# One encoder layer on one core: the mix as seven half-size products, and the first layer norm by token rows

## The chip, the cores and the metric

The kernel runs on one core of one Trainium2 chip. The metric is the device time of one execution, in microseconds (us); before the change the median of three runs is 2267.95 us (2264.13 to 2268.24). One execution was also taken by the hardware profiler, and all rows below come from it.

## The reference

One layer of a bidirectional encoder: 512 tokens, 2048 channels, everything in float32.

```python
proj = h @ w_in[i]                                   # 512x2048 @ 2048x4608
...                                                  # 8 windowed heads (oa), 8 dilated heads (ob)
ya = rms_norm(oa.reshape(b, s, A_Q), gn_a[i])
yb = rms_norm(ob.reshape(b, s, B_QKV), gn_b[i])
mix = jnp.concatenate([ya, yb], axis=-1) @ w_o[i]    # 512x2048 @ 2048x2048
h = layer_norm(ALPHA * h + mix, ln1_g[i], ln1_b[i])
ff = jnp.square(jax.nn.relu(h @ w1[i])) @ w2[i]      # 2048 -> 8192 -> 2048
ple = (p[i] @ w_ple[i]) * jax.nn.sigmoid(h @ w_ple_gate[i])
h = layer_norm(ALPHA * h + ff + ple, ln2_g[i], ln2_b[i])
```

## The kernel before

Each float32 operand is split into a rounded part (name ending in h, made by ScalarE with a Copy) and the rest (ending in l, made by VectorE with a subtract). A product is three matmuls: high by high, high by low, low by high.

**Phase 1** runs 36 projection units of 48 matmuls each; the attention heads are interleaved with them. Its weights come in pieces of 1024 columns that are split in halves of 512.

**The mix** follows: 16 output blocks on the windowed half `yA`, 16 on the dilated half `yB`, 24 matmuls a block, 768 in all, with channels on the partitions. The last head's work is strewn between the first blocks. `Norm` (`add`, `shift`, `take`, `stats`) gathers the first layer norm's sums during the second half: sums over channels are matmuls with a vector of ones (`col_sums`, L265), and a row of results is spread over the partitions by matmuls too (`spread`, L281). Then 96 matmuls of the PLE product run, `norm` scales the 16 blocks (L465, L466, L501), and SyncE stores them to `h_d` (L502).

**The gate, w1 and w2** use Strassen's scheme (`strassen`, L602): the product of tokens and weights is cut in halves of tokens (th), of contraction and of columns, and seven products of half size replace eight. One call handles half of the output columns: 28 steps of 12 matmuls of 512 columns, in the order of `STEPS`, an entry (product, contraction piece). VectorE makes the sums of weights that the products need (L616, L617, L625, L634) and the low halves (L599). The sums of activations, the factors, come from `h_factors` (L536), which reloads quarters of h from `h_d`, adds them and splits them (L545 to L574). A finished product is added into the output quarters it belongs to (`quarters`), and a full quarter goes to `gated`, which multiplies the sigmoid by the PLE quarter, turns h by matmuls with the identity (L694) and adds it (L695).

Gate is two such calls, w1 eight, w2 eight. The last w2 call feeds the second layer norm: `finish` (L761) runs once for each half of tokens, the half th=1 when product 4 ends, th=0 when product 2 ends, which is the last in `STEPS`.

Each engine works through its own list in order, and a dependent instruction holds up all behind it. Weights are loaded into rings of a few buffers: SyncE issues those of the rings "r" and "q", GpSimd those of "k".

## Time and profile before

| | before |
|---|---|
| median of 3 runs | 2267.95 us |
| the profiled execution, its own time | 2262.9 us |
| its span, first to last instruction | 2261.1 us |
| TensorE busy in the span | 2144.7 us (95%) |
| VectorE, ScalarE, GpSimd busy | 1612.5, 1061.6, 124.3 us |
| mean granted TensorE clock | 0.982 |

Names in the rows: PE is TensorE, PEld its weight load, DVE VectorE, ACT ScalarE, POOL GpSimd, SP SyncE. "a<-b" is output from inputs. Durations of neighbouring instructions overlap; the pitch, from one start to the next, is what an instruction costs in a row of equals.

### The profile page before, as it was taken

The page shows a single profiled execution, that of the slowest core. Times are in us where ns is not written, and L with a number is a line of the kernel's source. Part 1 is how long each engine was busy: PE and PEld are TensorE (multiplying, and loading weights), DVE is VectorE, ACT ScalarE, POOL GpSimd, SP SyncE. Part 2 cuts the span into 40 slices and gives each one's busy share as a digit, 9 for nine tenths or more (in the row PEclk, how much of TensorE's full clock was granted, in tenths as well). Part 3 has the DMA queues.
Part 4 walks back from the last instruction along what each step waited for, and adds up shares of the span by engine and source line. Part 5 has one row for each costly group of instructions (what it writes and reads, how often), then busy time and mean ns, then how long its engine had stood idle before and what let it go on. Part 6 is the DMA issues. An engine that isn't in the chain of part 4 may idle for free.

```text
span 2261.1 us, 26072 instructions
## 1 busy us (share of the span) xinstructions
PE 2144.7 (95%) x9672; PEld 1757.3 (78%) x9672; DVE 1612.5 (71%) x1969; ACT 1061.6 (47%) x1372; POOL 124.3 (5%) x192
## 2 busy tenths in 40 slices
PE   9999999999995799999999999998899999999994
PEld 7888888888884588888888888776777787787783
DVE  7666655566475988776876877777677776777787
ACT  5554444343234444454555455455445555455331
POOL 0000000000003000000000000000011011001000
PEclk9999999999998899999999999999999999999997
DMA  6212212224225775565565566567669679678552
GB/s 225 75 66 76 84 66 84 84 100 138 99 88 209 269 271 202 202 230 180 190 229 177 196 214 204 190 221 250 202 186 285 182 206 277 181 210 289 187 197 82
DMA packets 124544, 401.60 MB, mean 178 GB/s; under 512 B 13024, under 2 KB 24288, under 8 KB 124416
## 3 DMA queue, kind: packets, MB, share of 16 engines
q1 hardware_dynamic: 88544, 285.51, 36.7%
q0 software_dynamic: 23584, 85.06, 13.4%
q10 hardware_dynamic: 12288, 29.36, 3.5%
q8 instruction: 76, 1.25, 0.2%
q14 instruction: 52, 0.43, 0.1%
HBM read 329.63 MB, written 70.25 MB: 177 GB/s over the span
## 4 chain that ended last, share of the span: by engine, by line
PE 76%; DMA 9%; DVE 9%; issue 3%; ACT 2%; DVEq 0%; SPq 0%; ACTq 0%
PE u L72 9%; PE u L71 9%; PE a L656 9%; PE u L73 9%; PE a L653 9%; PE a L655 8%; DMA wr<-in_w 5%; PE b L656 4%; PE b L653 4%; PE b L655 4%; DVE wl L599 4%; PE c L656 2%; PE c L653 2%; PE c L655 2%; DMA qs<-s_d 2%
## 5 line engine op out<-in xcount | busy, mean ns | idle before, releaser
L598 ACT ACTIVATE wh<-wr 128x1024 fp32r<-128x1024 f32 x288 | 303.8, 1059 | 345.2 <-PE a L655 194.0
L599 DVE TENSOR_TENSOR wl<-wr,wh 128x1024 fp32r<-128x1024 f32 x288 | 350.2, 1221 | 96.5 <-ACT wh L598 93.3
L64 ACT ACTIVATE wh<-raw 128x512 fp32r<-128x512 f32 x216 | 135.7, 629 | 282.2 <-PE u L72 267.3
L65 DVE TENSOR_TENSOR wl<-raw,wh 128x512 fp32r<-128x512 f32 x216 | 150.8, 699 | 160.8 <-ACT wh L64 129.0
L598 ACT ACTIVATE wh<-wk 128x1024 fp32r<-128x1024 f32 x144 | 152.6, 1060 | 179.3 <-PE b L655 89.5
L71 PE MATMUL u<-xh,wh 128*128 128x512 f32 x576 | 227.8, 395 | 5.6 <-ACT xh L64 5.6
L73 PE MATMUL u<-xh,wl 128*128 128x512 f32 x576 | 225.7, 392 | 0.0
L72 PE MATMUL u<-xl,wh 128*128 128x512 f32 x576 | 225.6, 392 | 0.0
L599 DVE TENSOR_TENSOR wl<-wk,wh 128x1024 fp32r<-128x1024 f32 x144 | 175.6, 1222 | 66.2 <-ACT wh L598 66.1
L634 DVE TENSOR_TENSOR wk<-wr,wk 128x1024 f32<-128x1024 f32 x72 | 88.2, 1224 | 97.1 <-DMA wr<-in_w 91.2
L653 PE MATMUL a<-wh,s1h 128*128 128x512 f32 x288 | 114.8, 399 | 30.7 <-DMA qh<-h_d 29.3
L71 PEld LDWEIGHTS u<-xh,wh 128*128 128x128 f32 x576 | 108.9, 189 | 27.1 <-ACT xh L64 5.6
L653 PE MATMUL b<-wh,s5h 128*128 128x512 f32 x288 | 116.6, 405 | 12.1 <-ACT wh L598 12.1
L73 PEld LDWEIGHTS u<-xh,wl 128*128 128x128 f32 x576 | 108.7, 189 | 22.7
L656 PE MATMUL b<-wl,s5h 128*128 128x512 f32 x288 | 117.2, 407 | 9.3 <-DVE wl L599 9.3
L72 PEld LDWEIGHTS u<-xl,wh 128*128 128x128 f32 x576 | 108.9, 189 | 22.0 <-DVE xl L65 0.4
L656 PE MATMUL c<-wl,s2h 128*128 128x512 f32 x288 | 113.3, 393 | 6.0 <-DVE wl L599 5.7
L656 PE MATMUL b<-wl,s3h 128*128 128x512 f32 x288 | 113.5, 394 | 4.1 <-DVE wl L599 3.9
L656 PE MATMUL a<-wl,s1h 128*128 128x512 f32 x288 | 114.8, 399 | 2.4 <-DVE wl L599 2.4
L655 PE MATMUL b<-wh,s5l 128*128 128x512 f32 x288 | 115.5, 401 | 0.0
L653 PE MATMUL a<-wh,s7h 128*128 128x512 f32 x288 | 112.6, 391 | 2.9 <-ACT wh L598 2.9
L656 PE MATMUL a<-wl,s7h 128*128 128x512 f32 x288 | 113.0, 392 | 1.2 <-DVE wl L599 1.1
(243 smaller groups left out, 4933.4 us busy)
## 6 DMA issues: line engine op xcount, KB each, us to landing
wr<-in_w SPq DMA_DIRECT2D x192, 512.0 KB, 4.0
raw<-in_w_in SPq DMA_DIRECT2D x64, 512.0 KB, 3.6
wq<-in_w SPq DMA_DIRECT2D x64, 512.0 KB, 3.7
wk<-in_w POOLq DMA_DIRECT2D x64, 512.0 KB, 4.8
qs<-s_d SPq DMA_DIRECT2D x56, 512.0 KB, 4.9
z_d<-ev POOLq DMA_DIRECT2D x42, 512.0 KB, 7.2
raw<-in_w_o SPq DMA_DIRECT2D x32, 512.0 KB, 3.4
s_d<-f POOLq DMA_DIRECT2D x32, 512.0 KB, 5.2
```

The lines of the kernel that those rows point to most:

```text
L64: nc.scalar.activation(hi, src, AF.Copy)
L65: nc.vector.tensor_tensor(lo, src, hi.bitcast(F32), op=ALU.subtract)
L71: nc.tensor.matmul(o, wh, ah, start=start, stop=False)
L72: nc.tensor.matmul(o, wh, al, start=False, stop=False)
L73: nc.tensor.matmul(o, wl, ah, start=False, stop=stop)
L598: nc.scalar.activation(hi, t, AF.Copy)
L599: nc.vector.tensor_tensor(lo, t, hi.bitcast(F32), op=ALU.subtract)
L634: nc.vector.tensor_tensor(t2[k], b21[k], t2[k], op=ALU.subtract)
L653: nc.tensor.matmul(o, sh[:, i, x], wh[:, c], start=first and k == 0 and j == 0, stop=False, skip_group_check=skip)
L655: nc.tensor.matmul(o, sl[:, i, x], wh[:, c], start=False, stop=False, skip_group_check=skip)
L656: nc.tensor.matmul(o, sh[:, i, x], wl[:, c], start=False, stop=k == 3 and j == 1, skip_group_check=skip)
```

## The change

The mix becomes two more calls of `strassen`. For that the scaled attention outputs are stored to DRAM (`y_d`) and reloaded as quarters, and `h_factors` becomes `factors`, which takes any loader. The PLE product moves ahead of the mix, between the pieces of the last head's work. Each finished quarter of the mix lies with tokens on the partitions; `mixed` adds ALPHA times x (loaded as `xn`), takes statistics, and `norm_rows` normalises 16 blocks of 512 channels, which `turned` transposes by 64 matmuls with the identity and evicts with gain and bias. The results serve directly as factors for products 5, 1, 6 and 2 and are stored by GpSimd (16 stores of 512 KB, `z_d` and `h_d`); the other factors reload from `h_d`. The gate's first call uses the order `FIRST5`, which begins with product 5, and the mix's second and the last w2 call use `ENDS`, in which all of th=1 ends six steps before the end. In the gate, h no longer comes by transposes of `h_d`; the normalised rows are loaded with gain and bias, and VectorE rebuilds ALPHA*h by four more instructions and one add a quarter. All weight rings are shared by all phases, so phase 1 splits pieces of 1024 columns, the attention outputs lie in rings "g" and "k", and ring q of phase 1 has 12 buffers and not 14.

```diff
-    yA = [split(ot, "y", "x") for ot in oA]
-    for j in range(NT):
-        o = unit(w_o[0, j], yA, 8)
...
-    n1 = Norm(acc)
-    for j in range(NT):
-        n1.add(j, unit(w_o[1, j], yB, 8))
-    n1.stats()
...
+    embed(0)
+    V = v_split(V)
+    embed(1)
+    hd.turn()
+    embed(2)
+    ssB = hd.values(V, ssB, oB)
+    rB = rms_stats(ssB)
+    embed(3)
+    rms_scale(oB, rB, 8)
...
+            k = g0 + 2 * j
+            nc.sync.dma_start(y_d[k:k + 2].rearrange("k p s -> p k s"), o)
...
+    def turned(th, n):
+        z, g = zs[th, n], n % 2
+        nc.gpsimd.dma_start(z_d[th, n], z)
+        i = 2 * th + n // 2
+        ha[g, i] = x = s_tile("ha", {0: "s4h", 1: "s4l", 2: "s7h", 3: "s7l"}[i])
+        for b0 in (0, 2):
+            pt = ps.tile([P, 2, HS], F32, name="pt", tag="pt", bufs=2)
...
+                    nc.tensor.transpose(pt[:, b, t * P:(t + 1) * P], z[:, t, (b0 + b) * P:(b0 + b + 1) * P], ident)
...
+                nc.scalar.activation(x[:, b0 + b], pt[:, b], AF.Identity, bias=vec[:, 2, j:j + 1],
+                                     scale=vec[:, 1, j:j + 1])
+        nc.gpsimd.dma_start(h_d[g, i], x)
+
+    def norm_rows(th):
+        mv, r = row_stats(th)
+        for n in (0, 2, 1, 3):
+            for i in range(2):
+                z = zs[th, n][:, i]
+                nc.vector.tensor_scalar(z, z, mv[:, i, 0:1], r[:, i:i + 1], op0=ALU.subtract, op1=ALU.mult)
+            turned(th, n)
...
+        def mixed(th, nh, y, c=c):
+            n = 2 * c + nh
+            z = pair("xt", "g") if c == 0 else s_tile("xt", "s1h", (P, 2, S))
+            nc.scalar.dma_start(z, xn[th * HS:(th + 1) * HS, n * S:(n + 1) * S].rearrange("(t p) s -> p t s", p=P))
+            zs[th, n] = z if c == 0 else y
+            nc.vector.scalar_tensor_tensor(zs[th, n], z, ALPHA, y, op0=ALU.mult, op1=ALU.add)
+            take_stats(th, n, zs[th, n])
+            if c == 1 and all((th, m) in zs for m in range(4)):
+                norm_rows(th)
+        strassen(lambda k, q, c=c: w_o[c, q, k], sy, quarters(mixed, {(1, 0): "k"} if c else {}),
+                 between=mid if c == 0 else {}, steps=ENDS if c else FIRST1)
...
-                pt = ps.tile([P, S], F32, name="pt", tag="pt", bufs=2)
-                for b in range(4):
-                    nc.tensor.transpose(pt[:, b * P:(b + 1) * P], hk[:, b, i * P:(i + 1) * P], ident)
-                nc.vector.scalar_tensor_tensor(g[:, i], pt, ALPHA, g[:, i], op0=ALU.mult, op1=ALU.add)
+                nc.vector.scalar_tensor_tensor(z[:, i], z[:, i], ALPHA, gb[:, 0], op0=ALU.mult, op1=ALU.mult)
+                nc.vector.scalar_tensor_tensor(z[:, i], gb[:, 1], ALPHA, z[:, i], op0=ALU.mult, op1=ALU.add)
+            nc.vector.tensor_tensor(g, g, z, op=ALU.add)
             nc.scalar.dma_start(z_d[th, n], g)
...
+FIRST5 = ((5, 0), (5, 1), (5, 2), (5, 3), (1, 0), (1, 1), (1, 2), (1, 3), (2, 0), (6, 0), (6, 1), (6, 2), (6, 3),
...
+ENDS = STEPS[:12] + ((2, 0), (7, 0), (7, 1), (7, 2), (7, 3), (2, 1), (4, 0), (4, 1), (4, 2), (4, 3),
+                     (3, 0), (2, 2), (3, 1), (3, 2), (2, 3), (3, 3))
```

**The start of the mix, VectorE.** Before, after the last head's softmax (L231), VectorE's list holds the scaling of an output block (L372) and low halves of weights (L65), one for each half piece:

```order
L231 TENSOR_SCALAR e_4426<-e_4426,rd_4431 128x512
L372 SCALAR_TENSOR_TENSOR acc_4508<-acc_4508,u_4473 128x512
L65 TENSOR_TENSOR vl_4517<-s_4511,vh_4516 128x512
L65 TENSOR_TENSOR wl_4578<-raw_4559,wh_4577 128x512
L65 TENSOR_TENSOR wl_4630<-raw_4627,wh_4629 128x512
L65 TENSOR_TENSOR wl_4646<-raw_4627,wh_4645 128x512
L372 SCALAR_TENSOR_TENSOR acc_4555<-acc_4555,u_4520 128x512
```

Now, behind the inverse root, the scalings of the dilated heads' outputs (`o`, L326), weight sums (L535, L536), low halves (L87) and factors of the mix (`qh`, from L464 on) stand in one row:

```order
L326 SCALAR_TENSOR_TENSOR o_2239<-o_2239,vec_87,rb_4424 128x512 x2
L326 SCALAR_TENSOR_TENSOR o_2856<-o_2856,vec_87,rb_4424 128x512 x2
L326 SCALAR_TENSOR_TENSOR o_3455<-o_3455,vec_87,rb_4424 128x512 x2
L326 SCALAR_TENSOR_TENSOR o_4054<-o_4054,vec_87,rb_4424 128x512 x2
L87 TENSOR_TENSOR wl_4554<-wr_4551,wh_4553 128x1024
L87 TENSOR_TENSOR wl_4578<-wr_4497,wh_4577 128x1024
L535 TENSOR_TENSOR wr_4551<-wq_4682,wr_4551 128x1024
L536 TENSOR_TENSOR wk_4573<-wk_4573,wr_4497 128x1024
L87 TENSOR_TENSOR wl_4606<-wr_4515,wh_4605 128x1024
L536 TENSOR_TENSOR wk_4601<-wk_4601,wr_4515 128x1024
L464 TENSOR_TENSOR qh_4464<-qh_4464,qh_4462 128x1024
L536 TENSOR_TENSOR wk_4632<-wk_4632,wr_4533 128x1024
```

One more weight row follows, and then `s5l_4468`, the low half that product 5's first step needs. `wk_4573` lies in ring "k", whose four buffers hold the `o` of the rows above until their stores have landed.

**From the mix to the gate, VectorE.** Before, the inverse root (L277), three low halves of PLE weights (L65) and the scalings of 16 blocks follow each other:

```order
L277 SCALAR_TENSOR_TENSOR r_5934<-rt_5938,r_5934 128x4
L65 TENSOR_TENSOR wl_6060<-raw_6053,wh_6059 128x512
L65 TENSOR_TENSOR wl_6106<-raw_6103,wh_6105 128x512
L65 TENSOR_TENSOR wl_6110<-raw_6103,wh_6109 128x512
L465 TENSOR_TENSOR acc_4508<-acc_4508,s_5910 128x512
L466 SCALAR_TENSOR_TENSOR acc_4508<-acc_4508,vec_79,s_5948 128x512
```

Now, behind the normalising of the rows (L641), stand the factors of the gate made from SBUF (`s1l`, `s6l`, `s2l`), the fourth "k" sum (`wk_5966`), and a factor sum that waits for quarters reloaded from `h_d` (`qh_5955`, L478). `wl_5971` is the low half for product 5's last step:

```order
L641 TENSOR_SCALAR c01_5329<-c01_5329,mv_5757,r2_5762 128x512
L445 TENSOR_TENSOR s6l_5801<-ha_5577,s6h_5800 128x1024
L536 TENSOR_TENSOR wk_5966<-wk_5966,wq_5964 128x1024
L445 TENSOR_TENSOR s2l_5824<-ha_5807,s2h_5823 128x1024
L651 TENSOR_TENSOR ha_5620<-ha_5620,ha_5830 128x1024
L445 TENSOR_TENSOR s1l_5847<-ha_5830,s1h_5846 128x1024
L445 TENSOR_TENSOR s6l_5852<-ha_5620,s6h_5851 128x1024
L478 TENSOR_TENSOR qh_5955<-qh_5953,qh_5955 128x1024
L87 TENSOR_TENSOR wl_5971<-wq_5964,wh_5970 128x1024
```

So work for product 7, which starts at the call's fifteenth step (`qh_5955`), stands ahead of work for its fourth.

**The same place, TensorE.** Now the last matmul of the mix (into bank b) is followed by the 32 transposes of th=1 (`pt`), and the gate's first matmul comes behind them; the 32 of th=0 stand between product 5's matmuls:

```order
L569 MATMUL b_5099<-wl_5736,s3h_4759 128x512
L629 MATMUL pt_5559<-ident_80,xt_5055 128x128
L629 MATMUL pt_5566<-ident_80,xt_5055 128x128
L629 MATMUL pt_5559<-ident_80,xt_5055 128x128 x3
L629 MATMUL pt_5566<-ident_80,xt_5055 128x128 x3
L629 MATMUL pt_5578<-ident_80,c10_5529 128x128 x4
L629 MATMUL pt_5585<-ident_80,c10_5529 128x128 x4
L629 MATMUL pt_5602<-ident_80,xt_4940 128x128 x4
L629 MATMUL pt_5609<-ident_80,xt_4940 128x128 x4
L629 MATMUL pt_5621<-ident_80,c11_5279 128x128 x4
L629 MATMUL pt_5628<-ident_80,c11_5279 128x128 x4
L566 MATMUL b_5879<-wh_5889,s5h_5594 128x512
```

Before, the PLE product's 96 matmuls stood at this place, between the norm's sums and the gate's first matmul.

**The same place, GpSimd.** Before, it subtracted the mean from 12 blocks (L451) and then issued the gate's loads into ring k. Now the stores of normalised rows (L622) and of their turned form (L634) stand in its list, and the gate's fourth load into ring k, which is `wk_5966` above, behind those of th=1:

```order
L622 DMA z_d_78<-c10_5529 128x1024
L634 DMA h_d_76<-ha_5558 128x1024
L622 DMA z_d_78<-xt_4940 128x1024
L634 DMA h_d_76<-ha_5577 128x1024
L634 DMA h_d_76<-ha_5601 128x1024
L622 DMA z_d_78<-c11_5279 128x1024
L634 DMA h_d_76<-ha_5620 128x1024
L79 DMA wk_5966<-in_w_gate 128x1024
L622 DMA z_d_78<-xt_5093 128x1024
```

The stores of `h_d` from which `qh_5955` is reloaded stand on both sides of that load.

## Rows read from the trace of the kernel before

**Rows 1.** The page: span, busy time by engine, the chain that ended last.

```profile
span 2261.1 us, 26072 instructions
PE 2144.7 (95%) x9672; PEld 1757.3 (78%) x9672; DVE 1612.5 (71%) x1969; ACT 1061.6 (47%) x1372; POOL 124.3 (5%) x192
PE 76%; DMA 9%; DVE 9%; issue 3%; ACT 2%; DVEq 0%; SPq 0%; ACTq 0%
```

**Rows 2.** Stretches from the mix's start: busy by engine, granted clock, DMA share, GB/s.

```profile
499.10:681.90 182.80, 182.80 (x833) 151.96 (x832) 109.32 (x188) 61.58 (x105) 4.29 (x8) 1.00 0.30 102
681.90:711.00 29.10, 25.83 (x129) 21.25 (x127) 22.05 (x37) 13.01 (x23) 16.32 (x12) 1.00 0.36 136
711.00:740.20 29.20, 0.00 (x0) 0.00 (x0) 7.10 (x9) 12.94 (x19) 2.14 (x4) 0.56 0.92 339
740.20:800.00 59.80, 51.08 (x186) 37.92 (x187) 55.13 (x49) 31.25 (x31) 0.00 (x0) 0.87 0.74 253
800.00:920.00 120.00, 119.51 (x550) 98.05 (x549) 97.45 (x91) 57.32 (x55) 4.23 (x8) 1.00 0.70 245
835.00:919.60 84.60, 84.58 (x390) 69.35 (x388) 68.69 (x64) 39.36 (x39) 2.11 (x4) 1.00 0.66 232
2232.70:2261.10 28.40, 0.00 (x0) 0.00 (x0) 24.20 (x72) 0.00 (x0) 0.00 (x0) 0.58 0.39 148
```

**Rows 3.** Waits from 499 to 920 us: sum, count, longest.

```profile
PE a L653 <- DMA qh<-h_d: 29.3, 1, 29.3
PE s L281 <- DVE r L277: 3.2, 1, 3.2
```

**Rows 4.** TensorE's timeline: start, duration; a 512-column pitch, then the norm's small matmuls.

```profile
520.45 0.39 PE L71 MATMUL u<-yh,wh 128*128 128x512 f32 x1
520.68 0.39 PE L72 MATMUL u<-yl,wh 128*128 128x512 f32 x1
...
684.19 0.95 PE L265 MATMUL s<-ones,s 128*128 128x1 f32 x8
```

**Rows 5.** VectorE's timeline: 1024-wide pitch, small dependent operations, then the tail.

```profile
740.40 1.22 DVE L599 TENSOR_TENSOR wl<-wr,wh 128x1024 fp32r<-128x1024 f32 x1
741.53 1.22 DVE L556 TENSOR_TENSOR qh<-qh 128x1024 f32<-128x1024 f32 x1
...
688.51 0.16 DVE L277 SCALAR_TENSOR_TENSOR r<-rt,r 128x4 f32<-128x4 f32 x1
688.71 1.27 DVE L275 TENSOR_TENSOR rt<-r 128x4 f32<-128x4 f32 x1
...
2227.28 1.22 DVE L743 TENSOR_TENSOR zl<-zl,a 128x1024 f32<-128x1024 f32 x1 [0.63 <-PE a L656]
2228.54 1.29 DVE L746 BATCH_NORM_STATS2 bs<-zl 128x6 f32<-128x512 f32 x2
...
2254.51 1.28 DVE L778 SCALAR_TENSOR_TENSOR zf<-zf,r,gb 128x1024 f32<-128x1024 f32 x1
2255.71 1.41 DVE L778 SCALAR_TENSOR_TENSOR zl<-zl,r,gb 128x512 f32<-128x512 f32 x2
```

**Rows 6.** GpSimd's timeline where VectorE's small operations slow down.

```profile
688.67 3.72 POOL L451 TENSOR_TENSOR acc<-acc,ms 128x512 f32<-128x512 f32 x3 [128.55 <-DVE r L277]
```

**Rows 7.** Groups of instructions, 499 to 920 us: busy, mean ns, idle before.

```profile
L466 DVE SCALAR_TENSOR_TENSOR acc<-acc,vec,s 128x512 f32<-128x512 f32 x16 | 10.9, 744 | 0.1
L695 DVE SCALAR_TENSOR_TENSOR c<-pt,c 128x512 f32<-128x512 f32 x14 | 9.0, 682 | 0.1
L501 ACT ACTIVATE acc<-acc,vec 128x512 f32<-128x512 f32 x16 | 10.0, 708 | 0.4 <-DVE acc L465 0.4
```

**Rows 8.** DMA issues, 480 to 920 us: count, KB each, median us to landing.

```profile
qh<-h_d SPq DMA_DIRECT2D x14, 512.0 KB, 5.5
wk<-in_w_gate POOLq DMA_DIRECT2D x8, 512.0 KB, 7.2
z_d<-c ACTq DMA_DIRECT2D x7, 512.0 KB, 4.9
```

**Rows 9.** Phase 1: TensorE's only wait, and ScalarE's largest.

```profile
PE u L71 <- ACT xh L64: 5.6, 1, 5.6
ACT wh L64 <- PE u L72: 167.8, 99, 3.0
```

More of the change, by code (lines that the diff above doesn't have):

```diff
@@ L499, in block_kernel, with embed @@
-    for j in range(NT):
-        z, b = n1.norm(j, 1)
-        nc.scalar.activation(z, z, AF.Identity, bias=b)
-        nc.sync.dma_start(h_d[j], z)
-    p2.__exit__(None, None, None)
-    tpc.__exit__(None, None, None)
+        p_hl.append(split(r, "p", "q"))
+    def embed(g):
+        wh, wl = w_split(w_load(w_ple[g], "r"))
+        for th in range(2):
+            e = pair("pe", "g")
+            for i in range(2):
+                o = bank()
+                t = 2 * th + i
+                c = slice(t * P, (t + 1) * P)
+                for k in range(2):
+                    d = slice(k * S, (k + 1) * S)
+                    mm3(o, (p_hl[k][0][:, c], p_hl[k][1][:, c]), (wh[:, d], wl[:, d]), k == 0, k == 1)
+                nc.scalar.activation(e[:, i], o, AF.Copy)
+            nc.scalar.dma_start(ple_d[th, g], e)
@@ L534, in put, with factors @@
         sg[p] = hi, lo
-    def h_factors(g, sg):
+    def factors(load, sg):
         q = {}
@@ L674, in quarters, with take_stats, row_stats @@
         return read
-    sh = [{}, {}]
-    early, late = zip(*(h_factors(g, sh[g]) for g in range(2)))
-    for f in early[0]:
-        f()
-    mid = {1 + n: [f] for n, f in enumerate(early[1] + late[0] + late[1])}
+    bs = [st.tile([P, 4, nc.vector.BN_STATS_DIM], F32, name=f"bs{t}", bufs=1) for t in range(NQ)]
+    def take_stats(th, n, z):
+        for i in range(2):
+            nc.vector.bn_stats(bs[2 * th + i][:, n], z[:, i])
+    def row_stats(th):
+        mv = st.tile([P, 2, nc.vector.BN_AGGR_DIM], F32, name="mv")
+        for i in range(2):
+            nc.vector.bn_aggr(mv[:, i], bs[2 * th + i])
+        v = st.tile([P, 2], F32, name="v2")
+        nc.vector.tensor_scalar(v, mv[:, :, 1], LN_EPS, None, op0=ALU.add)
+        r = st.tile([P, 2], F32, name="r2")
+        rsqrt(r, v)
+        return mv, r
@@ new lines, in block_kernel @@
+    steps = list(zip(*(factors(load_y(g), sy[g]) for g in range(2))))
+    for f in steps[0] + (steps[1][0], steps[2][0], steps[1][1], steps[2][1]):
+        f()
+    mid = {5 + n: [f] for n, f in enumerate([s[0] for s in steps[3:]] + [s[1] for s in steps[3:]])}
+    for c in range(2):
+        def mixed(th, nh, y, c=c):
[9 more added lines that the diff above has]
+                 between=mid if c == 0 else {}, steps=ENDS if c else FIRST1)
@@ L682, in block_kernel, with load_h, load @@
+    def load_h(g):
+        def load(i, x):
+            nc.sync.dma_start(x, h_d[g, i])
+        return load
+    steps = [factors(load_h(g), sh[g])[4:] for g in range(2)]
+    mid = {3 + 2 * n: [f] for n, f in enumerate(steps[0] + steps[1])}
     for c in range(2):
@@ L748, in read @@
                     nc.gpsimd.dma_start(z_d[q[0], q[1]], z[q])
+            if p in LAST:
+                ends.append(q[0])
+                if c == 1 and ends.count(q[0]) == 2:
+                    finish(q[0], z)
             if c == 1 and p == 5:
@@ L812 @@
 LAST = (2, 3, 7, 4)
-ON_VECTOR = (0, 4, 8, 12)
-W_SLOTS = 10
-RAW = 4
 PI2 = []
```

416 lines of the change are left out of this document (175 added, 241 removed).

## The prediction

> **What bounds the kernel now.** I read the page first. TensorE is busy 95% of the span and holds 76% of the chain that ended last [rows 1]: time is saved by fewer matmuls, or by shorter stretches in which TensorE stands still. So I cut the time from the mix's start to the gate's end into stretches, and read beside them what TensorE waited for. In the mix TensorE is busy throughout, and VectorE 109 of 183 us. Between the last PLE matmul and the gate's first there are 29.2 us without one matmul, while the DMA engines move 339 GB/s [rows 2]; the one long wait there is for the quarters of h reloaded from `h_d` [rows 3]. In the next 59.8 us only 186 matmuls run and VectorE is busy 55.1 us [rows 2]: VectorE is the bound there. From 800 us on TensorE is full again.
>
> A matmul of 512 columns follows its predecessor by 0.227 us, and eight small ones of the norm's sums take 0.95 us, 0.12 each [rows 4]. A 1024-wide operation of VectorE costs 1.135 us in a row of equals, a small dependent one 0.20 us [rows 5]. A 512-wide one is taken at 0.68 us [rows 7].
>
> **TensorE's work.** 768 matmuls of the mix become 2 x 28 x 12 = 672: 96 x 0.227 = 21.8 us less. The norm's sums and spreads go, 48 rows of 0.12: 5.7 us less. The gate's 64 transposes go and 64 of the normalised rows come: zero. The PLE's 96 matmuls only move. Together -27.5 us.
>
> **Waits that go.** 29.3 for `h_d` and 3.2 for the inverse root [rows 3]; 59.8 - 186 x 0.227 = 17.6 in the stretch bound by VectorE, in which the granted clock was 0.87; 0.5 after it [rows 2]. Together 50.6 us.
>
> **Waits that come.** All are on VectorE's list, whose order is fixed.
>
> 1. The inverse root of the dilated heads' norm now stands between weight work: 12 small operations (2.4 us) with six 1024-wide ones (6.8). TensorE has 11 PLE matmuls left behind the sums, 2.5 us. Wait 6.7 us. Before, the same chain stood under the mix's first half and cost nothing.
>
> 2. The mix's start. Product 1 covers four steps, 48 x 0.227 = 10.9 us. Product 5 needs `s5l_4468`, which stands behind `wk_4573`, whose buffer of ring k is free when the first `o` is stored. From the spread: an eviction of 0.7 and two scalings at 0.74 [rows 7], a store like the 4.9 us of `z_d<-c`, a load like the 7.2 us of `wk` [rows 8], 14.3 in all; then seven 1024-wide operations, 7.9. 22.2 - 10.9 = 11.3 us. Behind it the 24 operations that make the mix's factors keep VectorE ahead of no step until product 7: following the list against steps of 2.7 us, I find 5.7 more. Together 17. A count bounds it: VectorE's list for the mix's first call (the inverse root included) is 99 us by these prices, TensorE's 76.2. Less the 2.5 covered, points 1 and 2 cannot be under 20; one more landing of 7.2 on the chain makes 31. I take 23.7.
>
> 3. The first layer norm. From the mix's last matmul VectorE has, until `s5l_5595` lets product 5 run, 8 operations of 1024 (9.1), four statistics (two take 1.29 us [rows 5], 2.6), 16 small ones (3.2), nine normalisations of 512 at 0.68 (6.1), and 0.6 of hand-over as at 2227.28 [rows 5]: 21.6 us, of which 32 transposes fill 3.8. Wait 17.8. If the normalisations take two thirds, 15; if ScalarE's 16 evictions (128x256, estimated at half of L501's 0.708 [rows 7]) are not hidden, 23.5. I take 17.8. A lowered clock behind these waits has no term of its own: at the gate's start of before it is part of the 17.6, and VectorE, not the matmuls, ends last there.
>
> 4. The gate's first call. `wl_5971`, for product 5's fourth step, comes 12 wide operations and seven normalisations after `s5l_5595`, 18.4 us; TensorE has three steps and 32 transposes for it, 12.0. With the following low halves, also late, 7.5 us. The reload for `qh_5955` is hidden there: turned quarter, store and load (7.2 and 5.5 [rows 8]) are due some 3 us before VectorE gets to it. Bounds 3 and 12.
>
> 5. The gate's second call. VectorE was busy 68.7 us in before's [rows 2]; per quarter four 512-wide operations and an add come and two go, 2.5 us, 10 in the call: 78.7 against TensorE's 76.2. With some unevenness 4 us (0 to 8).
>
> 6. The last head's softmax now has only 24 PLE matmuls above it, and loads may be late elsewhere in the mix: 3.3 us (0 to 6).
>
> Together 56.3 us, 5.7 more than go. A check from the other side: VectorE's list from that inverse root to the gate's last add is 353 us by these prices, TensorE's work 313; so points 1 to 5 cannot be under about 37, and my 53 leaves VectorE idle for 16.
>
> **The tail.** Before, VectorE still has 24.2 us of work after the last matmul and 4.0 follow for the output [rows 2]. With `ENDS` one half of `finish` stands ahead of the last two low halves. Left after the last matmul: 3.4 of that half, two sums 2.3, statistics 2.9, `finish` twice 5.0 (1.20 and two at 0.70, for two row blocks [rows 5]) and 1.5 of small ones, then 4.0 and 0.6 of hand-over, 24.5 us for 28.4: -3.9.
>
> **Costed at nothing.** Phase 1 does the same matmuls and its pieces are only wider. TensorE waited there once, for 5.6 us at the start; ScalarE waited 167.8 us for buffers that TensorE held [rows 9], so splits run ahead by that much. In w1 and the earlier w2 calls the lists of all engines are the same but for a swap.
>
> Sum: -27.5 + 5.7 - 3.9 = -25.7 us. The profiled execution of 2262.9 would be 2237; the median of the runs shown is 5 above it, so I forecast 2242.
>
> **A rule against it.** When GpSimd subtracts (688.67 [rows 6]), VectorE's small operations take 1.27 us and not 0.16 [rows 5]; those subtractions go. GpSimd now issues 16 stores while VectorE normalises. If it is held up as VectorE was, for eight normalisations (8 x 0.68 = 5.4 us), the reload of point 4 has 3 us of cover and 2.4 us fall on TensorE: 2244. The Trainium skill, "SBUF — State Buffer", section "Who interferes with whom", says that VectorE and GpSimd share a port pair as an exclusive lock, and that a tensor_scalar in a two-port mode keeps GpSimd from writing the descriptors of its DMAs. The trace agrees on the lock (1.27 against 0.16 us); no run here shows a delayed store.
>
> **Rivals.** (a) The forecast, 2234 to 2253: chance 0.60. (b) VectorE hardly idles, and waits fall to 37 + 3.3: 16 us less, 2226. For it: at the same kind of start, after 740 us, VectorE was busy 55.1 of 59.8 us [rows 2]. Against it: `wk_4573` waits for a store and a load. 0.12. (c) VectorE stands idle at loads: each microsecond beyond 16 is one of the span. For it: before's gate start, where 339 GB/s and 29.2 us went into loads [rows 2], and the mix's start now moves stores, reloads and weights at once. At 26 to 37 idle it gives 2252 to 2263, 0.09; at about 40 the change does not do what it says, 2266, 0.07. (d) The held-up stores, 2244: 0.05. (e) Slower: phase 1 has wider pieces, three buffers of split halves, attention outputs in the weight rings and two fewer in ring q. If each of the 36 units waits 1 us, 36 us come: 2278. It decides from 30 / 36 = 0.84 us a unit. Against it is the 167.8 us above. 0.07.
>
> **Numbers.** The runs of before spread over 4 us, so 0.2% (4.5 us) is about what can be told from no change. Faster: 0.60 + 0.12 + 0.09 + 0.05 = 0.86; same 0.07; slower 0.07. The range 2227 to 2263 leaves out the lower half of (b), the "same" part of (c) and (e), 0.20. The likeliest case alone spans 2234 to 2253.
>
> **What would show it.** In the new profile: TensorE's rows fall by 96 wide ones; the wait of the first `b<-wh,s5h` of the mix is on `s5l` or ring k and near 11 us; the wait of the gate's first product is 15 to 23 us and ends on VectorE, not on `h_d`; the gate's windows have VectorE over 95% busy; phase 1 still ends near 499 us plus the moved PLE; the tail is 24 to 25 us. The forecast is wrong if the two starts cost much over 45 us together, or if TensorE waits in phase 1.

## The result

The changed kernel takes 2282.26 us, the median of 4 runs (2279.21 to 2287.26); the kernel before, run beside it, takes 2267.86 (2264.13 to 2268.24). The ratio is 1.0069, interval 1.0048 to 1.0091: slower by 0.7%, where 2242 and faster was forecast. The profiled execution took 2283.15 us, 46 more than the 2237 that the sum gave for it.

The page of the changed kernel answers to [rows 1]: span, busy time by engine, and the chain that ended last by engine and by line.

```profile
span 2281.4 us, 25611 instructions
PE 2156.5 (95%) x9528; PEld 1743.6 (76%) x9528; DVE 1663.9 (73%) x1890; ACT 1074.0 (47%) x1300; POOL 112.9 (5%) x188
PE 71%; DMA 11%; DVE 11%; issue 4%; ACT 2%; DVEq 0%; SPq 0%; ACTq 0%
PE a L569 9%; PE a L566 9%; PE a L568 9%; PE u L93 6%; PE u L94 6%; PE u L95 6%; PE b L569 5%; PE b L568 5%; PE b L566 5%; DVE wl L87 4%; DMA wr<-in_w 3%; DMA qs<-s_d 2%; DMA gb<-in_lnb 2%; PE c L569 2%; PE c L566 2%
```

TensorE issues fewer matmuls and is nevertheless busy 12 us longer; its share of the chain that ended last falls from 76 to 71%, and a load that the gate did not have before, `gb<-in_lnb` (the first layer norm's gain and bias, for the gate's quarters), holds 2% of that chain alone. The stretches of the changed kernel answer to [rows 2]. They are: PLE and last head; the mix's two calls; the layer norm; the gate's first call; its second; w1's first; w1's second; the tail.

```profile
499.70:542.25 42.55, 31.90 (x148) 25.18 (x148) 20.82 (x42) 22.56 (x39) 0.00 (x0) 0.93 0.56 203
542.25:716.90 174.65, 163.00 (x672) 129.14 (x672) 153.75 (x152) 76.97 (x75) 5.88 (x11) 0.96 0.72 244
716.90:735.70 18.80, 7.26 (x33) 5.19 (x33) 17.99 (x40) 9.62 (x18) 5.19 (x9) 0.68 0.70 256
735.70:829.80 94.10, 87.75 (x369) 69.21 (x370) 80.39 (x79) 54.85 (x63) 6.39 (x12) 0.94 0.80 268
829.80:922.10 92.30, 79.87 (x328) 63.00 (x326) 73.18 (x72) 37.51 (x37) 2.12 (x4) 0.93 0.71 228
922.10:1017.30 95.20, 87.02 (x372) 69.84 (x371) 70.33 (x64) 41.55 (x44) 2.12 (x4) 0.95 0.55 187
1017.30:1098.40 81.10, 81.10 (x370) 66.12 (x368) 59.96 (x52) 41.37 (x45) 4.27 (x8) 1.00 0.60 201
2258.20:2281.40 23.20, 0.00 (x0) 0.00 (x0) 18.50 (x35) 0.00 (x0) 0.00 (x0) 0.61 0.43 164
```

A call has 336 matmuls of 512 columns, 76.2 us at 0.227. Before, the gate's second call lasted 80.9 us, of which its transposes took some 4, and w1's first 80.1, at a clock of 1.00 ([rows 2] has 835 to 919.6 us). Now they last 92.3 and 95.2 at 0.93 and 0.95, and only w1's second call runs at full clock again. These two calls are 26.5 us longer than before and 27 over the forecast, although the gate's second call has no transposes any more. These are the stretches before:

```profile
838.70:919.60 80.90, 80.89 (x374) 66.31 (x372) 65.03 (x61) 37.95 (x37) 2.11 (x4) 1.00 0.65 228
919.60:999.70 80.10, 79.69 (x367) 65.88 (x365) 59.30 (x53) 39.77 (x43) 2.11 (x4) 1.00 0.53 183
```

What TensorE waited for, in the changed kernel, first from the PLE to the gate's start, then in the gate and w1's first call (sum, count, longest):

```profile
PE b L566 <- ACT s5h L444: 10.9, 2, 5.7
PE s L306 <- DVE r L302: 6.1, 1, 6.1
PE pt L629 <- DVE xt L641: 4.4, 1, 4.4
PE a L569 <- DVE wl L87: 2.6, 1, 2.6
PE a L566 <- ACT rb L322: 2.2, 1, 2.2
PE u L93 <- ACT ph L73: 1.9, 1, 1.9
...
PE u L95 <- DVE pl L74: 0.5, 1, 0.5
```

```profile
PE b L569 <- DVE wl L87: 12.2, 4, 5.8
PE a L569 <- DVE wl L87: 6.0, 1, 6.0
PE b L566 <- ACT s5h L444: 5.7, 1, 5.7
PE c L569 <- DVE wl L87: 4.9, 3, 2.4
PE b L566 <- ACT wh L86: 3.3, 1, 3.3
```

The wait of 5.7 for `s5h`, at the gate's first matmul, stands in both lists; the one at product 5 of the mix is the other 5.3. In the second list TensorE waits most for `wl`, the low halves of weights. VectorE's list has something else ahead of them, which the waits of all engines from 820 to 1017 us name:

```profile
DVE zn L693 <- DMA gb<-in_lnb: 17.5, 5, 6.7
...
ACT wh L86 <- DVE zn L694: 8.0, 2, 5.6
ACT c L690 <- DVE c L584: 7.3, 3, 5.3
```

VectorE stood at the gain and bias of a finished quarter, five times. Its own timeline at the end of the gate's second call shows two of these, and what is queued behind:

```profile
914.54 1.22 DVE L87 TENSOR_TENSOR wl<-wr,wh 128x1024 fp32r<-128x1024 f32 x1 [0.21 <-ACT wh L86]
921.18 1.29 DVE L693 SCALAR_TENSOR_TENSOR zn<-zn,gb 128x512 f32<-128x512 f32 x2 [5.42 <-DMA gb<-in_lnb]
922.39 1.28 DVE L694 SCALAR_TENSOR_TENSOR zn<-gb,zn 128x512 f32<-128x512 f32 x2
923.60 2.35 DVE L87 TENSOR_TENSOR wl<-wr,wh 128x1024 fp32r<-128x1024 f32 x2
...
930.41 1.21 DVE L87 TENSOR_TENSOR wl<-wr,wh 128x1024 fp32r<-128x1024 f32 x1
935.01 0.69 DVE L693 SCALAR_TENSOR_TENSOR zn<-zn,gb 128x512 f32<-128x512 f32 x1 [3.39 <-DMA gb<-in_lnb]
```

5.4 and 3.4 us idle, each with weight work of the next call behind it. Each finished quarter asks for three loads (`pl`, `zn`, `gb`), all in ring "g", all issued from ScalarE's list; before, there were two (`pl`, `hk`).

### The profile page after: what moved, and what is told of

It reads as the page before. It is cut to its first block, busy times and chain, and to the rows that moved or that the text cites. A ratio compares the mean times of both kernels' runs of the same rounds, so it can differ in the third digit from the quotient of the medians.

```text
span 2281.4 us, 25611 instructions
## 1 busy us (share of the span) xinstructions
PE 2156.5 (95%) x9528; PEld 1743.6 (76%) x9528; DVE 1663.9 (73%) x1890; ACT 1074.0 (47%) x1300; POOL 112.9 (5%) x188
## 4 chain that ended last, share of the span: by engine, by line
PE 71%; DMA 11%; DVE 11%; issue 4%; ACT 2%; DVEq 0%; SPq 0%; ACTq 0%
PE a L569 9%; PE a L566 9%; PE a L568 9%; PE u L93 6%; PE u L94 6%; PE u L95 6%; PE b L569 5%; PE b L568 5%; PE b L566 5%; DVE wl L87 4%; DMA wr<-in_w 3%; DMA qs<-s_d 2%; DMA gb<-in_lnb 2%; PE c L569 2%; PE c L566 2%
## 5 line engine op out<-in xcount | busy, mean ns | idle before, releaser
L86 ACT ACTIVATE wh<-wr 128x1024 fp32r<-128x1024 f32 (+1 forms) x400 | 415.3, 1042 | 562.0 <-PE a L568 222.1
L87 DVE TENSOR_TENSOR wl<-wr,wh 128x1024 fp32r<-128x1024 f32 (+1 forms) x400 | 477.4, 1198 | 223.3 <-ACT wh L86 218.5
L86 ACT ACTIVATE wh<-wk 128x1024 fp32r<-128x1024 f32 x160 | 169.6, 1060 | 201.7 <-PE a L568 99.1
L87 DVE TENSOR_TENSOR wl<-wk,wh 128x1024 fp32r<-128x1024 f32 x160 | 194.5, 1220 | 67.8 <-ACT wh L86 67.1
L569 PE MATMUL c<-wl,s2h 128*128 128x512 f32 x320 | 128.4, 401 | 9.8 <-DVE wl L87 9.7
L566 PE MATMUL a<-wh,s7h 128*128 128x512 f32 x320 | 127.0, 397 | 3.2 <-ACT wh L86 1.7
L566 PE MATMUL a<-wh,s6h 128*128 128x512 f32 x320 | 125.5, 392 | 3.2 <-DVE zl L743 2.1
L566 PE MATMUL c<-wh,s2h 128*128 128x512 f32 x320 | 127.8, 399 | 0.0
L568 PE MATMUL c<-wh,s2l 128*128 128x512 f32 x320 | 127.6, 399 | 0.0
L568 PE MATMUL b<-wh,s3l 128*128 128x512 f32 x320 | 127.4, 398 | 0.0
```

The lines of the kernel that those rows point to most:

```text
L86: nc.scalar.activation(hi, t, AF.Copy)
L87: nc.vector.tensor_tensor(lo, t, hi.bitcast(F32), op=ALU.subtract)
L566: nc.tensor.matmul(o, sh[:, i, x], wh[:, c], start=first and k == 0 and j == 0, stop=False, skip_group_check=skip)
L568: nc.tensor.matmul(o, sl[:, i, x], wh[:, c], start=False, stop=False, skip_group_check=skip)
L569: nc.tensor.matmul(o, sh[:, i, x], wl[:, c], start=False, stop=k == 3 and j == 1, skip_group_check=skip)
```

## The experiments

"With `hk`" below is the changed kernel whose gate gets h as before, by 64 transposes of `h_d`, without the loads of `zn` and `gb` and without the eight stores of normalised rows. The gate's first call, its second and w1's first take 281.6 us in the changed kernel; this sum of the three is the measure below where the gate is meant. When an edit adds, takes out or moves an instruction, the builder orders the engines' lists near that place anew. In the three runs with pads alone, and from the run with `hk` to its padded ones, the records of every engine stand in the same order. Elsewhere some 20 to 75 records of VectorE's list moved or went, so such a run changes a load or an operation and, with it, the order of its neighbours.

**Where the operands lie.** Matmuls whose stationary operand was factor 2, 3 or 4 stood 0.233 us apart and not 0.227: product 3 here, six pitches in 1.40 us.

```profile
1143.05 0.39 PE L566 MATMUL b<-wh,s3h 128*128 128x512 f32 x1
...
1143.28 0.40 PE L568 MATMUL b<-wh,s3l 128*128 128x512 f32 x1
...
1144.45 0.39 PE L566 MATMUL b<-wh,s3h 128*128 128x512 f32 x1
```

Over all matmuls of 512 columns, what the pitches between 0.227 and 0.30 have above 0.227 sums to 27.2 us (called the excess below), and to 4.6 in the kernel before. The pool of these factors begins at an address that is 224 modulo 256, the weights' halves lie at 64; before, all lay at 192. Three runs moved pools by padding and did nothing else; this is the edit of the first.

```diff
+    pad = ctx.enter_context(tc.tile_pool(name="pad", bufs=1, side="right"))
+    pad.tile([P, 8], F32, name="pad")
```

> The changed kernel with 32 bytes of padding on the right side of SBUF and nothing else: every tile there (factors of products 2, 3 and 4, attention operands) moves from an address of 32 modulo 64 to one of 0; the order of instructions on every engine stays. Theory A (addresses slow TensorE): matmuls whose weights are those factors go from a pitch of 0.233 us back to 0.2265 us; the excess of 27 us over all matmuls in the changed kernel's trace falls to about the 4 us of the kernel before. Stretches that VectorE bounds give nothing back, so the time falls by 8 to 23 us, to 2259 to 2274. Theory B (the slow pitch only follows stalls): pitch and time stay, 2282 within 4 us.

2281.31 us, ratio 1.0064 (1.0047 to 1.0081); the excess is 22.5 us, and the three factors still cost 5 to 6 ns a matmul more. Their distance is now a multiple of 64 but not of 256: a distance modulo 64 does not decide.

The kernel before, with its factors moved by 32 bytes and its weights' halves by 64:

```diff
+    pd1 = tc.tile_pool(name="pd1", bufs=1)
+    pd1.__enter__().tile([P, 8], F32, name="pd1")
...
+    pd2 = tc.tile_pool(name="pd2", bufs=1)
+    pd2.__enter__().tile([P, 8], F32, name="pd2")
```

> The kernel before, with its pool of factors (all seven products) moved by 32 bytes and the other pools left at multiples of 64; the order of instructions stays. Theory A: all 28 steps of each of the 18 calls go to a pitch of 0.233 us, 6048 matmuls by 0.0065 us, 39 us, less what VectorE-bound calls absorb: 25 to 39 us more, 2293 to 2307. Theory B: the same time as before, within 4 us.

2280.4 us, 1.006 (1.0046 to 1.0074), with every engine's order unchanged; the excess is 38.7 us, all seven factors at +6 ns, a call of w1 82.0 us for 80.8. So two pads of 32 bytes, and nothing else, make the kernel before as slow as the changed one. Theory A had said 25 to 39 us, and 14 came: of 34 us of added excess, 20 did not reach the time. The control leaves out the second pad, so that all operands move by 32 together:

> The kernel before with factors and all rings moved by the same 32 bytes, where the earlier run moved them apart. Theory A1 (difference of the two addresses): pitch 0.227 us as in the kernel before and its time, 2266 within 4 us. Theory A3 (each operand must start at a multiple of 64): pitch 0.233 us and 2280 within 4 us.

2267.45 us, 0.9997 (0.9988 to 1.0006), excess 5.6: it is the distance between the two operands, not either one's own alignment.

**The gate's way to h.**

```diff
-        nc.gpsimd.dma_start(z_d[th, n], z)
...
-            z = pair("zn", "g")
-            nc.scalar.dma_start(z, z_d[th, n])
-            gb = pair("gb", "g")
+            hk = block("hk")
+            nc.scalar.dma_start(hk, h_d[n % 2, 2 * th + n // 2])
```

> The changed kernel with the gate's old way of adding h: the quarter of h is reloaded from DRAM and turned by TensorE, two VectorE operations a quarter in place of five, no load of gain and bias and no store of the normalised rows. Theory A (the gate's loads through ring g and ScalarE's list, and VectorE's extra work, cost the two gate calls and the first w1 call): those three, 94.2 + 92.3 + 95.2 us in the changed kernel's profile, fall to about 90 + 83 + 82, 27 us less, 2255. Theory B (slowness there is from addresses or from the start of the gate): under 8 us less, 2274 to 2282.

2261.17 us, 0.9979 (0.9966 to 0.9991). The gate's second call and w1's first are at full clock again, and the three calls sum to 259.4:

```profile
831.60:912.90 81.30, 81.30 (x373) 66.55 (x372) 65.08 (x62) 38.02 (x37) 2.12 (x4) 1.00 0.66 232
912.90:993.80 80.90, 80.78 (x366) 65.96 (x366) 59.40 (x52) 39.98 (x43) 2.12 (x4) 1.00 0.55 182
sum 259.40, PE 252.02 PEld 203.40 DVE 206.73 ACT 134.77 POOL 8.50; mean PE 84.01 PEld 67.80 DVE 68.91 ACT 44.92 POOL 2.83
```

22.2 us less, and 21.1 of the median, although TensorE has 64 transposes more (7.7 us at 0.12 each): this one part of the change costs more than its whole loss of 14.4. With `hk` and the 32-byte pad:

> Both edits together: the padding and the gate's old way of adding h. If both theories A hold and their stretches hardly overlap: 2282 less 15 less 27, 2236 to 2245, faster than the kernel before by 1 to 1.4%. If only one holds: 2255 to 2270. If neither: 2282.

2259.0 us, 0.9967 (0.9953 to 0.998), not to be told from the run without the pad. With `hk` and 160 bytes, which puts the factors at 64 modulo 256 like the halves:

> The kernel of the run with both edits (gate's old way, padding), with 160 bytes of padding in place of 32: the factors of products 2, 3 and 4 now lie at the same residue of 256 (64) as the weight halves that TensorE streams against them; with 32 bytes they lay at 192 against 64. Order unchanged. Theory A1 (the two addresses must agree modulo 256): their pitch falls from 0.2327 to 0.227 us, the excess over all matmuls from 23 to about 5 us, the time from 2259 to 2243 to 2253. Theory A2 (the upper region of SBUF, whatever the residue): pitch and time stay, 2259 within 4 us.

2259.78 us, 0.9955 (0.9941 to 0.9969). The pitch is cured, excess 5.9 us; of product 3 now nine pitches take 2.04 us, 0.227 each:

```profile
1117.73 0.39 PE L568 MATMUL b<-wh,s3h 128*128 128x512 f32 x1
...
1119.77 0.39 PE L568 MATMUL a<-wh,s7h 128*128 128x512 f32 x1
```

But of the 23 us of pitch almost nothing reaches the time. From w1's second call to the last matmul it takes 1241.9 us and the changed kernel 1240.9 (before 1232.7); in 480 us of w1 the transposes (L711) wait 7.2 us for VectorE, and in the changed kernel 2.8. In the changed kernel the excess from w1's second call on is 15 us above before's and TensorE's idle time 5.5 below it; with the pitch cured, TensorE is idle 47.8 us there and before 40.5. What the pitch gave went into waits: theory A1 had the pitch right and the time, 2243 to 2253, wrong.

**Loads or VectorE's work.** The changed kernel without the load of gain and bias; the PLE tile stands in for it, so the residual is wrong:

```diff
-            gb = pair("gb", "g")
-            nc.scalar.dma_start(gb, bass.AP(tensor=lnb.tensor, offset=lnb.offset + n * S, ap=[[0, P], [D, 2], [1, S]]))
+            gb = e
```

> The changed kernel without the gate's load of gain and bias; the PLE quarter stands in for them, so that VectorE's operations stay as they are (what is left out: the true gain and bias in the gate's sum). One load and one buffer of ring g fewer a quarter. Theory L (late loads through ring g and ScalarE's list hold VectorE): the second gate call and the first w1 call fall from 92 + 95 to about 84 + 82, 21 us, to 2261. Theory W (VectorE's extra work bounds them): under 6 us less, 2276 to 2282.

2273.65 us, 1.0017 (1.0008 to 1.0027); three calls 273.6. The 8.6 us lie between the two theories. VectorE now stands at `zn<-z_d`, 11.8 us: the next load of the three.

All three loads, but two of the five operations on them (most of the residual sum is left out):

```diff
-            for i in range(2):
-                nc.vector.scalar_tensor_tensor(z[:, i], z[:, i], ALPHA, gb[:, 0], op0=ALU.mult, op1=ALU.mult)
-                nc.vector.scalar_tensor_tensor(z[:, i], gb[:, 1], ALPHA, z[:, i], op0=ALU.mult, op1=ALU.add)
-            nc.vector.tensor_tensor(g, g, z, op=ALU.add)
+            nc.vector.scalar_tensor_tensor(z[:, 0], z[:, 0], ALPHA, gb[:, 0], op0=ALU.mult, op1=ALU.mult)
+            nc.vector.scalar_tensor_tensor(g[:, 0], z[:, 0], ALPHA, g[:, 0], op0=ALU.mult, op1=ALU.add)
```

> The changed kernel with all the gate's loads, but two of the five operations that rebuild h a quarter left, which read each loaded tile once (what is left out: most of that sum). 2.5 us of VectorE a quarter fewer. Theory L: under 8 us less, 2274 to 2282, since the loads still come late. Theory W: 92 + 95 fall to about 83 + 82, 20 us or more, to 2255 to 2262.

2282.54 us, 1.0065 (1.0052 to 1.0077); three calls 280.2, and the wait at `gb` rises from 17.5 to 23.5 us. The time gains nothing, but the three calls do not stay as they were: the two that had lost take 89.7 and 86.3, 11.5 less, and the gate's first takes 104.2, 10 more, with VectorE at `gb` for 12.8 us between 733 and 838 us and not 5.4.

The three loads issued by SyncE and not from ScalarE's list (`nc.scalar.dma_start` to `nc.sync.dma_start`, three times):

> The changed kernel with the gate's loads of PLE quarter, normalised rows, and gain and bias issued by SyncE in place of ScalarE; all else stays. Theory Q (a load that waits for a buffer of ring g holds up ScalarE's list, and with it the high halves of weights): the second gate call and the first w1 call, 92.3 + 95.2 us in the changed kernel, lose 8 us or more together and the time falls to 2274 or less. Theory R (the ring itself is too small: three buffers a quarter out of four, so loads start late whoever issues them): those two stay within 5 us of 187.5, the time 2278 to 2286.

2271.19 us, 1.0021 (1.0011 to 1.0031). w1's first call falls from 95.2 to 86.1, the gate's second does not (92.8). Together they lose 8.6 us, and the time is under 2274, as theory Q said: ScalarE's list delays the last quarters' loads, and is a part only.

One load of three with all of VectorE's operations kept (the PLE tile stands in for both others; the residual is wrong):

```diff
-            z = pair("zn", "g")
-            nc.scalar.dma_start(z, z_d[th, n])
-            gb = pair("gb", "g")
-            nc.scalar.dma_start(gb, bass.AP(tensor=lnb.tensor, offset=lnb.offset + n * S, ap=[[0, P], [D, 2], [1, S]]))
+            z = gb = e
```

> The changed kernel (2282.3 us) with only one of the three loads that each finished quarter of the gate starts: the PLE tile also stands in for the normalised rows and for gain and bias. All of VectorE's and ScalarE's operations stay. Left out: the true residual in the last sum. Leaving out one of these loads gave 9 us before. Theory L (the second gate call and the first w1 call lose their 31 us to the three loads through the shared ring and ScalarE's queue, and to nothing else): both calls fall to 80 to 84 us each, the time by 20 to 27, to 2255 to 2262. Theory W (the five added VectorE operations per quarter cost as well): one of the calls stays above 86 us and the time above 2265.

2268.21 us, 1.0004 (0.9994 to 1.0014); both calls stay above what theory L said:

```profile
832.10:919.90 87.80, 79.93 (x338) 64.00 (x337) 74.78 (x72) 37.39 (x38) 2.11 (x4) 0.96 0.53 180
919.90:1005.70 85.80, 82.46 (x362) 66.38 (x361) 65.34 (x61) 40.08 (x43) 2.11 (x4) 0.98 0.53 175
sum 269.60, PE 251.57 PEld 201.17 DVE 224.92 ACT 133.49 POOL 10.58; mean PE 83.86 PEld 67.06 DVE 74.97 ACT 44.50 POOL 3.53
```

Two loads less take 12.0 of the 22.2 us; 10.2 remain, and VectorE no longer waits for a quarter's loads. From 833 to 862 us, and again from 916 to 950, it is busy with no idle time above 0.3 us:

```profile
839.16 1.28 DVE L691 SCALAR_TENSOR_TENSOR pl<-pl 128x512 f32<-128x512 f32 x2
840.36 0.68 DVE L690 SCALAR_TENSOR_TENSOR pl<-pl 128x512 f32<-128x512 f32 x1
840.97 1.22 DVE L692 TENSOR_TENSOR c<-c,pl 128x1024 f32<-128x1024 f32 x1
842.10 0.68 DVE L691 SCALAR_TENSOR_TENSOR pl<-pl 128x512 f32<-128x512 f32 x1
842.70 1.22 DVE L87 TENSOR_TENSOR wl<-wr,wh 128x1024 fp32r<-128x1024 f32 x1
```

TensorE's one long wait of this call is for the `wl` of the last row:

```profile
843.97 0.79 PE L569 MATMUL b<-wl,s5h 128*128 128x512 f32 x1 [5.41 <-DVE wl L87]
```

Ahead of it stand the operations of two quarters. At the pitches of these rows a quarter has 4 x 0.60 + 1.13 - 2 x 0.60 = 2.33 us more work than with `hk`; four of the eight quarters end at the two turns between calls, 9.3 us. In the gate's second call and w1's first TensorE stands idle 11.2 us, in the version with `hk` 0.1 us. Its waits above 0.3 us there (5.4, 0.6, 1.9 and 3.0) are all for `wl`, and ahead of each VectorE has had no idle time above 0.3 us for over 10 us. So theory W holds for this part, and most of the idle time has the size of the added work. That the other 12.0 are the loads alone, theory L, is likely by the waits at `gb` and `zn`, but not shown apart from the order that moved with them.

**The first calls.** In the version with `hk` and 160 bytes the mix's first call takes 94.5 us, the gate's 97.6. Twelve sums of factors left out (L480, L485, L486; the products get wrong factors):

```diff
-            nc.vector.tensor_tensor(q[2], q[0], q[2], op=ALU.subtract)
...
-            nc.vector.tensor_tensor(q[1], q[1], q[3], op=ALU.subtract)
-            nc.vector.tensor_tensor(q[1], q[1], q[2], op=ALU.add)
```

> The version with the gate's old way and 160 bytes of padding, in which the factors of products 7 and 3 are split without their sums (what is left out: three sums for each half of the contraction, 6 of 24 factor operations of VectorE in the mix's first call and 6 in the gate's first; the loads stay). Theory V (both first calls are bound by VectorE's work): each call loses 4 to 7 us of its 94.5 and 97.6, the time falls from 2260 to 2246 to 2252. Theory D (they are bound by loads, stores and the order of the list): under 2 us a call, 2256 to 2262.

2257.49 us, 0.9958 (0.9943 to 0.9973); calls 93.7 and 98.7. So these sums do not set the calls. But they stand behind the longest waits, which stay (6.3 us for product 5's factors in the mix, 7.0 for `wh` in the gate); VectorE's work ahead of those was not varied. In the gate's first call of the version with `hk` and 160 bytes TensorE waits for

```profile
PE a L568 <- ACT wh L88: 6.6, 1, 6.6
PE b L568 <- ACT s5h L446: 5.0, 1, 5.0
```

and the `wh` of the first row stands on ScalarE's list behind the evictions of the transposes and the high halves of factors: ScalarE is busy 14.95 of the 15.75 us ahead of it. The same sums on GpSimd (`nc.vector` to `nc.gpsimd` in the three lines):

> The same version with those 12 factor sums on GpSimd in place of VectorE, nothing left out. Theory V and a free GpSimd: most of the run without the sums is kept, 2248 to 2256. Rival: GpSimd takes some 2.8 us for each (1.4 us for 512 columns in the kernel before), and slows VectorE's two-input operations while it runs, so that the first calls gain nothing: 2258 to 2266.

2281.48 us, 1.006 (1.0047 to 1.0073); calls 103.6 and 110.0, worse than the rival said. A sum takes GpSimd 2.4 to 3.6 us and VectorE 1.2.

The gate's late factors from rows stored long ago (their values are then wrong):

```diff
-            nc.sync.dma_start(x, h_d[g, i])
+            nc.sync.dma_start(x, y_d[4 * g:4 * g + 4, :, (i // 2) * HS:(i // 2 + 1) * HS].rearrange("k p t -> p k t"))
```

> The version with the old residual and the aligned pools (2259.8 us; gate's first call 97.6 us for 76.2 of matmuls), with one edit: the quarters that the gate's four late factors are made of are loaded from y, which was stored over 40 us earlier, and not from the turned rows that have just been stored. Left out: the gate's late factors get wrong values, so the gate's sums are wrong; every instruction and every byte stays. Theory R (the first call waits for the chain of a quarter turned, stored and loaded again): the call falls to 82 to 88 us and the time by 9 to 15, to 2245 to 2251. Theory O (the order and length of VectorE's and ScalarE's lists set the call, the loads are ready in time or nearly so): the call stays within 2 us of 97.6 and the time at 2258 to 2262.

2256.7 us, 0.9957 (0.9942 to 0.9972); the call falls by 2.9 to 94.7, and the wait for `wh` from 6.6 to 4.3. The versions that share this code have the call at 96.5 to 98.3, so some 2 us are clear of their spread; the time does not tell it from none. The mix's quarters from the input x (the mix then multiplies x):

```diff
-            nc.sync.dma_start(x, y_d[k0:k0 + 4, :, c].rearrange("k p t -> p k t"))
+            nc.sync.dma_start(x, xT[k0:k0 + 4, :, c].rearrange("k p t -> p k t"))
```

> The same version with one edit in the mix: the quarters of the attention output are loaded from the kernel's input x, which lies in DRAM from the start, and not from y, which the norm has just stored. Left out: the mix multiplies x in place of the normalised attention output; every instruction and every byte stays. The mix's first call takes 94.5 us for 76.2 of matmuls. Theory R: the loads can come as soon as the ring has room, the call falls to 80 to 86 us and the time by 9 to 15, to 2245 to 2251. Theory O: the call falls by 3 us at most, the time stays at 2256 to 2262.

2262.95 us, 0.9974 (0.9963 to 0.9986); the mix's first call grows to 99.7. Neither theory had a longer call, and the run does not decide between them, since VectorE's list changed: the factor sum for product 5 moved up, and `s5l` starts at 553.0 us and not at 561.7. With that the waits for product 5's factors, 5.2 and 1.5 us, are gone; VectorE stands 4.05 us at a load of `wk` instead, and TensorE waits 12.7 us for halves of weights and not 2.7. The order of VectorE's list decides where the mix's first call waits. And the late factors made later, in the same version:

```diff
-    mid = {3 + 2 * n: [f] for n, f in enumerate(steps[0] + steps[1])}
+    mid = {}
+    for n, f in zip((8, 10, 12, 13, 15, 17), steps[0] + steps[1]):
+        mid.setdefault(n, []).append(f)
```

> The version with the old residual and the aligned pools (2259.8 us) with the six steps that make the gate's late factors moved in the lists of all engines: they stand ahead of steps 8, 10, 12, 13, 15 and 17 of the gate's first call and no longer 3, 5, 7, 9, 11 and 13. Nothing else changes, and the values are the reference's. If ScalarE's and VectorE's lists stand behind a reload that isn't there yet (theory R, 4 to 10 us), the wait goes as the reload gets some 10 us more: the call 88 to 93 us, the time 2250 to 2256. If the order is not what holds the call (theory O: the total of VectorE's work), it stays within 2 us of 97.6; if the factors now come too late themselves, the call and the time grow by 3 to 8 us.

2255.74 us, 0.9949 (0.9933 to 0.9966); the call takes 94.6, which neither theory had, and its wait for `wh` falls to 4.7. This version and the one that it was made from (0.9955) are the fastest here that compute the reference; the two cannot be told apart.

**The tail.** The same version with the last w2 call in the order `STEPS`:

```diff
-                     STEPS if more or c == 0 else ENDS)
+                     STEPS)
```

> The same version with the old order of steps in the last w2 call, so that half of the second layer norm no longer ends six steps before the end. My step on the tail (3.9 us from that order): TensorE's last matmul to the end of the span takes 28 us and not 23 to 24, the time rises from 2260 to 2263 to 2266. Rival (the low halves behind that norm hold TensorE up by as much as the tail gains): the last w2 call gets shorter by 3 us or more, the time stays within 1.5 us.

2259.76 us, 0.9961 (0.9945 to 0.9976). The tail grows from 23.6 to 27.1 us, and the time does not move by what can be measured. The rival did not come either: the last w2 call takes 76.3 us for 76.9. `ENDS` shortens the tail as planned, but 3.5 us are too few for these runs to show in the time.

## Why the prediction was wrong, point by point

Stage by stage, against the working above:

- **TensorE's work**: right in number, 9672 to 9528 rows, but not in pitch (next to last point).
- **Waits that go**: they went; the PLE begins at 499.7, where the mix began at 499.1 before, and TensorE's longest wait from there to w1 is 6.1 us and not 29.3.
- **Point 1**, 6.7: 6.1 for `r`, and 2.2 more for the spread's eviction `rb`. 1.6 over.
- **Point 2**, 17: the first call is 19.8 over its 76.2, the second 2.2. 5 under-sized. The wait at product 5 came, but at 5.3 and 1.5 us and not near 11. From the first scaling to that sum VectorE is busy 13.7 of 16.5 us, with 0.9 idle at `wk` and 0.6 at the reloaded quarter: what stands ahead of `s5l` is its list more than the loads. The other 13 us of the 19.8 are smaller waits (1.4, 2.6), matmuls at the lower clock and pitch.
- **Point 3**, 17.8: 18.8 us pass, of which 32 transposes fill 3.8 by the price given there: 15.0. Over-sized by 2.8. The normalisations were taken at 0.68; in the rows below two take 0.99 and pairs follow each other after 0.91, 0.46 each: nine of them, 2.0 us less, most of the 2.8. The point named this case, two thirds, as its lower one; its terms give 15.8 there and not 15.
- **Point 4**, 7.5: 94.2 less 76.2 and 3.8 for the second half of the transposes leaves 14.2, 6.7 over. The reload called hidden accounts for up to 3 of it, by the run that loads y instead.
- **Point 5**, 4 (0 to 8): this is the step that failed. The second call is 16.0 over its matmuls, 12 more than said, and w1's first, under "costed at nothing" with all of w1, 15.1 longer than before's 80.1. The step had the right operations and set them against the call as a whole: 78.7 us of VectorE for 76.2 of TensorE. That total was too high, since its 68.7 covers 84.6 us; in the call's own 80.9 us VectorE was busy 65.0, and it is busy 73.2 in the changed call, 79% of it, where the prediction named over 95% as its sign (the gate's first call has 85%). So VectorE has less work than TensorE there, and TensorE waits all the same. The quarters end in pairs at the turn of a call, where VectorE also makes the next call's first halves and sums: in the run with one load it has no idle time at these turns, and TensorE stands idle 11 us in the two calls, near the 9.3 us of added work. And the added loads, `zn` and `gb`, were listed in the change and not priced: ring "g" and ScalarE's list bring them late and VectorE stands in front of them with the next call's `wl` behind it (17.5 us at `gb`; the run with two loads less gained 12 in the three calls). That the new way to h costs all of this, 21 us, is shown by the run with `hk`; the split between work and loads is less firm. Work taken out alone gave 0 in the time: 11.5 us less in these two calls and 10 more in the gate's first.
- **Point 6**, 3.3: in the first list of waits above, point 1's rows aside, the PLE's stretch has 1.9 for `ph` and 0.5 for `pl`, 2.4 in all. 0.9 under.
- **The tail**, 24.5 (the terms, with `finish` at two times 5.0, make 24.7): 23.2, 1.3 under.
- **Clock**: "a lowered clock behind these waits has no term of its own" was wrong. In the four calls with waits, 21, 14, 12 and 17 matmuls follow each other at 0.43 us, which is the lower of the two levels (a granted clock of 0.5); the kernel before has 23 of them in the gate's first call and none in the next two. 41 more at 0.2 us are 8 us, inside the sizes above: a wait of 5 us cost more than 5.
- **w1 and w2 at nothing**: from w1's second call to the last matmul 8 us more. In the changed kernel the pitch alone is more than that, but curing it leaves the 8 us as waits. 5 of the 7 us of added idle time in the cured version lie in w1's last call and w2's first, where TensorE's longest wait, for `wh`, is 9.2 us and before 6.9. What makes it longer is not settled.

These make 1.6 + 5.0 - 2.8 + 6.7 + 12.0 + 15.1 - 0.9 - 1.3 + 8.0 = 43.4 us over the forecast, of the 46. Of the rivals, (c) came nearest in kind, VectorE idle at loads, but at another place: it was priced at the two starts, and it happened at the gate's end. (d) did not happen: two stores issued while VectorE normalises take 0.74 us on GpSimd and the one behind them 0.53, so two stores lose 0.2 us each and not 5.4 in all. These are GpSimd's and VectorE's rows of the changed kernel there:

```profile
721.98 0.74 POOL L622 DMA_DIRECT2D z_d<-xt  x1 [27.32 <-DVE xt L641]
722.89 0.74 POOL L622 DMA_DIRECT2D z_d<-c  x1 [0.17 <-issue]
724.90 0.53 POOL L634 DMA_DIRECT2D h_d<-ha  x1 [1.28 <-ACT ha L632]
```

```profile
721.60 0.99 DVE L641 TENSOR_SCALAR c<-c,mv,r 128x512 f32<-128x512 f32 x2
722.51 0.99 DVE L641 TENSOR_SCALAR xt<-xt,mv,r 128x512 f32<-128x512 f32 x2
```

The Trainium skill, "SBUF — State Buffer", "Who interferes with whom", says that operations of VectorE in a two-port mode, which `tensor_scalar` can enter, keep GpSimd from writing the descriptors of its DMAs. The direction agrees with these rows, 0.74 against 0.53 us; what it cost here is 0.4 us, and the whole reload behind it is worth 3 at most. (e) did not happen; phase 1 ends 0.6 us later. The rest of the change, with h taken as before, is worth 0.2% as it stands and 0.45 to 0.5% with the pools aligned: 5 to 12 us of the 25.7 forecast. What bounds the two first calls (of the mix 18 to 20 us over its matmuls, of the gate 11 to 15 when its transposes are taken off at 0.12) stays open in part. The traces show where they wait: at product 5's factors behind VectorE's list in the mix, at the layer norm's first factor and behind ScalarE's list in the gate. Moved orders shifted these waits and shortened a call by 3 us at most; how short a call could get by a better order was not tried.
